# A two-layer diffusion step on one core: DeltaNet rounds whose TensorE order is written down, and a first norm from token-major square sums

## The chip, the cores and the metric

The kernel runs on one core of a Trainium2 chip. The metric is the device time of one launch in microseconds; smaller is better. TensorE (PE in the profile, its weight loads PEld), VectorE (DVE), ScalarE (ACT), GpSimd (POOL) and SyncE (SP, here only a DMA queue) run side by side and wait for each other through semaphores.

## The reference

One inference step of a trunk with two layers over 640 tokens: 128 context tokens and 512 latent tokens, model width 1024. Layer 0 is grouped-query attention, layer 1 is a bidirectional gated DeltaNet with 8 heads; each layer ends in a squared-ReLU MLP. What matters here:

```python
def trunk_layer(x, mods, gain1, gain2, w1, w2, mixer):
    shift1, scale1, gate1, shift2, scale2, gate2 = mods
    mix, aux = mixer(rms_norm(x, gain1) * (1 + scale1) + shift1)
    x = x + gate1 * mix
    h = rms_norm(x, gain2) * (1 + scale2) + shift2
    x = x + gate2 * (jnp.square(jax.nn.relu(h @ w1)) @ w2)
    return x, aux
...
def modulation(cond, w_mod, b_mod):
    m = jax.nn.silu(cond) @ w_mod + b_mod          # w_mod: 1024 x 6144 for each layer
...
def delta_mixer(h, s0, w_in, conv_w, a_log, dt_bias, norm_gain, w_out):
    proj = h @ w_in                                 # q, k, v, z: 8 heads x 128 each
    qkv = silu(centred_depthwise_conv(qkv, conv_w)) # 5 taps
    ...                                             # per head and direction: decay matrices,
    tinv = triangular_solve(eye + lower, eye)       # the inverse of a triangular matrix,
    S, o = lax.scan(step, s0, ...)                  # and a scan over chunks of tokens
```

## The kernel before

Activations stand feature-major: 8 tiles of 128 features by 640 tokens. Every weight and activation that enters a large matmul is split into a rounded part (hi, on ACT) and a rest (lo, on DVE or POOL), and each product is three matmuls (`mm3`). A projection of 128 outputs is done in two halves of 320 tokens, 24 matmuls each (`dense_half`, `dense_steps`).

**Order of the work.** The program is written as generators that `weave` interleaves: it always advances the part whose next step is the smallest share of its declared number of steps. This gives the written order. At build time a planner goes through the instructions with its own costs and puts each engine's instructions in an order: when an engine comes free in its plan, the earliest-written instruction that is ready then goes first. So an engine's order can differ from the written one; on the chip each engine then runs its queue strictly in that order. A `NoSync` edge between two instructions fixes their order on the engine and adds no wait.

**The start** (`run`, stage "ps0"). Five token tiles of `x` (`load_x`, 512 KB each) and then the first third of layer 0's modulation weights (`modulate(0, 0)`: 8 steps of 1 MB, each as four 256 KB pieces into free slots, `fetch_slots`) come over SP's queue. `transpose_x` turns `x` feature by feature on PE, DVE copies it out of PSUM, ACT squares it, DVE adds the squares; then a matmul with a column of ones, a reciprocal square root on DVE (`finish_rstd`) and a broadcast by matmul give the first norm's factor. These steps are written alternately with the 8 modulation steps. `key_weights` loads and splits the key weights (L559) and the first query weight (`q0`). `first_norm` multiplies by the factor (`us`), finishes the modulation, and makes h for three token segments (128, 256, 256 tokens): for every third feature tile on POOL, else on DVE. The key projection then takes one block of 128 tokens after another (24 matmuls each); block 0 needs segment 0, blocks 1 and 2 segment 1, blocks 3 and 4 segment 2.

**The DeltaNet rounds** (`delta`). Round r does, woven together: the projections of head r (`dn_dense`, declared 54 steps of three matmuls, rounds 0 to 7), the decay matrices of head r-1 (`dn_decay`, 20 steps), the inverse of head r-2 (`dn_inverse`, 10 steps), the scan of head r-3 (`dn_scan`, 14 steps), and from round 6 on the z projections (`gated`). Two hand-overs go through DRAM: `dn_decay` computes k times k on PE (its tenth step), DVE makes `gm` of it, writes it out (`gmd`), reads its diagonal blocks back (`ptmp`), solves them in 28 small dependent operations (`ptri`), writes the result (`td`), and `dn_inverse` of the next round reads it with 16 DMAs on SP's queue (`wide`, L1102). The first matmuls of an inverse (`big<-wide,a`) wait for that; they are written as the third of its ten steps. Rounds 8 to 10 have no q, k, v projection.

Of the kernel before, what the change touches and what calls it, by code (L numbers as in the profile page):

```python
# [2 lines left out]

# [5 lines left out]
F32 = mybir.dt.float32  # L9
F32R = mybir.dt.float32r  # L10
I32 = mybir.dt.int32
AF = mybir.ActivationFunctionType
ALU = mybir.AluOpType
AX = mybir.AxisListType

P = 128
# [61 lines left out]
def weave(*parts):  # L78
    live = [[0, n, i, g] for i, (g, n) in enumerate(parts)]
    while live:  # L80
        live.sort(key=lambda e: ((e[0] + 1) / e[1], e[2]))
        e = live[0]
        try:
            next(e[3])
            e[0] += 1
        except StopIteration:
            live.pop(0)
# [5 lines left out]
def pinned(tc, main, n, side, m):  # L93
    nc = tc.nc
    last = {}
    why = mybir.DependencyInfo(mybir.DependencyClass.NoSync, mybir.DependencyReason.DATA)
    traced = lambda i: nc.cur_bb.bb.instructions[i:]
    at = len(traced(0))
    done = step = 0
    for _ in main:  # L100
        step += 1
        for i in traced(at):
            if i.engine in PINNED:
                last[i.engine] = i.name
        at = len(traced(0))
        while done * n < step * m and next(side, True) is None:
            done += 1
            for i in traced(at):
                if i.engine in last:
                    tc.add_manual_dep(i, last[i.engine], why, reason="paced")  # L110
            at = len(traced(0))
    drain(side)


def drain(g):
    for _ in g:
        pass


class Model:  # L120
# [340 lines left out]
            out += [r[:, 0, :], r[:, 1, :]]  # L461
        return out

    def fetch_slots(self, src):
        out = []
        for i in range(4):
            r = self.main("h" if i < 2 else "a", shape=[P, 512])
            self.nc.sync.dma_start(out=r, in_=src[:, i * 512 : (i + 1) * 512])
            out.append(r)
        return out  # L470

    def load_x(self):
# [6 lines left out]
            xs.append(t)  # L479
        return xs  # L480

    def transpose_x(self, xs, x):
        for f in range(FT):
            x.append(self.main("x"))
            ps = self.ps("big", 2, 1024)
            for b in range(NBLK):
                self.tr(ps[:, b * P : (b + 1) * P], xs[b][:, f * P : (f + 1) * P])
            self.nc.vector.tensor_copy(out=x[f], in_=ps[:, :T])
            sq = self.main("x")
            self.act(sq, x[f], AF.Square)  # L490
            if f == 0:
                acc = sq
            else:
                self.tt(acc, acc, sq, ALU.add)
            yield
        cols = self.ps("nps", 1)[:, :NBLK]
        for b in range(NBLK):
            self.mm(cols[:, b : b + 1], acc[:, b * P : (b + 1) * P], self.one_col)
        r = self.finish_rstd(cols)
        out = self.ps("big", 2, 1024)  # L500
        for b in range(NBLK):
            self.mm(out[:, b * P : (b + 1) * P], r[:, b : b + 1].to_broadcast([P, P]), self.ident)
        self.r0 = out[:, :T]
        yield

    def first_norm(self, x, gm):
        us = [self.main("a") for _ in range(FT)]
        for f in range(FT):
            self.tt(us[f], x[f], self.r0, ALU.mult)
        drain(gm)  # L510
        h = self.new_h()
        gain, mods = self.gains[0][0], self.mods[0]
        for s, e, g in FIRST:
            for f, (hi, lo) in enumerate(h):
                eng = self.nc.gpsimd if f % 3 == 2 else self.nc.vector
                u = us[f][:, s:e]
                self.ts(u, u, gain[:, f, g : g + 1], ALU.mult, mods[:, f, g : g + 1], ALU.add, eng=eng)
                self.act(hi[:, s:e], u, AF.Copy)
                self.tt(lo[:, s:e], u, hi[:, s:e].bitcast(F32), ALU.subtract, eng)
        return h  # L520

    def spill(self, x, eng=None):
# [49 lines left out]
    def key_weights(self):  # L572
        v, g = self.nc.vector, self.nc.gpsimd
        self.kw = self.kv_weights(self.kv_raw(QW), lambda: self.wtile([P, 4, 256]), 4, (g, v))
        self.vraws = self.kv_raw(QW + KVH * P)
        self.q0 = self.pair(self.a["attn_w_in"][0], 0, 0, eng=g)

    def attn_kv(self, h, x):
        nc, a = self.nc, self.a
# [181 lines left out]
    def psum(self, name):  # L761
        return self.tc.tile_pool(name=name, bufs=1, space=bass.MemoryType.PSUM)
# [481 lines left out]
    def delta(self, h, first):  # L1244
# [31 lines left out]
        for r in range(HEADS + 3):  # L1276
# [11 lines left out]
                parts.append((self.dn_dense(h, r, first if r == 0 else None), 54))  # L1288
            if r >= HEADS:
                parts.append((islice(wm, MODS[r - HEADS]), MODS[r - HEADS]))  # L1290
            weave(*parts)
        drain(wm)
        self.first = self.prefetch(a["dn_w_out"][0], 0, [f * P for f in range(FT)])
        drain(self.dn_out(HEADS - 1))
# [27 lines left out]
    def run(self):  # L1322
# [1 line left out]
        pool = lambda name: tc.tile_pool(name=name, bufs=1)  # L1324
        psum = self.psum
        FC = [f * P for f in range(FT)]
        with psum("ps0") as self.pq:
            xs = self.load_x()
            self.setup()
            gm = self.modulate(0, 0, self.fetch_slots)  # L1330
            x = []
            tx = self.transpose_x(xs, x)
            for _ in range(FT):
                next(gm)
                next(tx)
            drain(tx)
            self.columns()
            self.key_weights()
            h = self.first_norm(x, gm)
        with pool("attn") as self.ph:  # L1340
            self.attention(h, x)
            first = self.prefetch(a["attn_w_out"][0], 0, FC)
# [126 lines left out]
```

## Time and profile before

| what | value |
|---|---|
| time, median of 3 runs | 1884.3 us (1880.81 to 1886.86) |
| profiled execution: its own time | 1883.34 us |
| profiled execution: span of the instructions | 1881.5 us |
| granted TensorE clock, mean | 0.984 |
| PE busy, share of the span | 95% |
| DMA traffic | 248.84 MB, mean 132 GB/s |

The profile is one execution. Busy time of an engine is the union of its instructions; a matmul's end is modelled, so a busy PE can still lose time between dependent matmuls. "Idle before" is the time an engine stood still just ahead of an instruction, with what ended it. Times in the trace count from the start of the span.

### The profile page before, as it was taken

To read this page: it belongs to the slowest core of one execution; us is meant where nothing else is said; L and a number is where in the kernel's file an instruction comes from. 1 tells how busy PE (TensorE), PEld (TensorE's weight loads), DVE (VectorE), ACT (ScalarE), POOL (GpSimd) and SP (SyncE) were. 2 spreads that over 40 slices of the span, in tenths; PEclk is the share of its full clock that TensorE was granted. 3 is DMA by queue.
4 is the path that set the end of the run, shared out by engine and by line. 5 is a ranking of instruction groups with operands and counts; after the bars stand their busy time and mean duration, and the time that the engine had idled before them with its cause. 6 is when DMAs were issued, how large, how long until landed. Compare 5 with 4: busy or idle time off the path is not lost.

```text
span 1881.5 us, 31040 instructions
## 1 busy us (share of the span) xinstructions
PE 1793.3 (95%) x11981; PEld 1657.3 (88%) x11981; DVE 991.3 (53%) x2294; ACT 753.9 (40%) x1725; POOL 311.6 (17%) x404
## 2 busy tenths in 40 slices
PE   6899999999999999999999999999899999999997
PEld 2778876979999999999898999776699999999997
DVE  4636662724454545556788876543664334343432
ACT  2445552523342433436766555533343223131331
POOL 1344221400010010142121101210251000000012
PEclk9899999999999999999999999999999999999998
DMA  7651127465676676624432332654721222222211
GB/s 279 217 161 49 34 85 219 112 201 165 189 224 196 198 227 180 200 82 165 130 105 81 106 109 85 192 169 143 230 81 48 74 79 74 73 79 75 72 46 56
DMA packets 289065, 248.84 MB, mean 132 GB/s; under 512 B 44847, under 2 KB 246982, under 8 KB 288918
## 3 DMA queue, kind: packets, MB, share of 16 engines
q1 hardware_dynamic: 269072, 207.85, 36.9%
q0 software_dynamic: 9136, 32.18, 4.7%
q10 hardware_dynamic: 10710, 6.83, 1.2%
q8 instruction: 94, 1.54, 0.3%
q14 instruction: 53, 0.43, 0.1%
HBM read 199.00 MB, written 45.20 MB: 130 GB/s over the span
## 4 chain that ended last, share of the span: by engine, by line
PE 75%; DVE 14%; DMA 5%; issue 2%; ACT 2%; POOL 1%; SPq 1%; POOLq 0%; ACTq 0%; DVEq 0%
PE dense L173 32%; PE pd L173 29%; PE scan L173 3%; PE big L173 2%; DVE cv L166 2%; PE mod L408 2%; DVE ptmp L160 2%; PE pd L408 2%; PE big L176 1%; DVE ptri L1069 1%; DVE a L160 1%; DMA raw<-in_w_mod 1%; DVE wide L160 1%; DMA ptmp<-gmd 1%; PE S L173 1%
## 5 line engine op out<-in xcount | busy, mean ns | idle before, releaser
L173 PE MATMUL pd<-h,w 128*128 128x320 f32 x2016 | 353.6, 320 | 10.3 <-ACT cv L163 6.2
L173 PE MATMUL dense<-a,wx 128*128 128x320 f32 x2238 | 338.4, 310 | 2.2 <-ACT wx L163 1.5
L173 PEld LDWEIGHTS dense<-a,wx 128*128 128x128 f32 x2238 | 331.6, 189 | 5.1 <-ACT wx L163 2.4
L173 PEld LDWEIGHTS pd<-h,w 128*128 128x128 f32 x2016 | 301.0, 190 | 37.0 <-issue 21.0
L163 ACT ACTIVATE wx<-raw 128x1024 fp32r<-128x1024 f32 x132 | 139.8, 1059 | 362.5 <-PE dense L173 214.7
L173 PE MATMUL dense<-h,wx 128*128 128x320 f32 x1776 | 266.9, 309 | 0.0
L173 PEld LDWEIGHTS dense<-h,wx 128*128 128x128 f32 x1776 | 261.7, 188 | 5.9 <-issue 5.0
L160 DVE TENSOR_TENSOR wx<-raw,wx 128x1024 fp32r<-128x1024 f32 x127 | 159.1, 1255 | 155.4 <-ACT wx L163 155.4
L173 PE MATMUL pd<-a,wx 128*128 128x320 f32 x1284 | 194.3, 309 | 0.0
L173 PEld LDWEIGHTS pd<-a,wx 128*128 128x128 f32 x1284 | 189.9, 188 | 0.0
L173 PE MATMUL pd<-h,wx 128*128 128x320 f32 x1008 | 152.0, 309 | 0.0
L166 DVE SCALAR_TENSOR_TENSOR x<-dense,c,x 128x192 f32<-128x192 f32 (+2 forms) x147 | 59.6, 433 | 175.3 <-PE dense L173 175.3
L173 PEld LDWEIGHTS pd<-h,wx 128*128 128x128 f32 x1008 | 148.8, 188 | 1.7 <-DVE a L160 1.7
L160 POOL TENSOR_TENSOR x<-x,half 128x320 f32<-128x320 f32 x48 | 54.1, 1127 | 526.1 <-ACT half L163 525.3
L163 ACT ACTIVATE a<-half 128x320 fp32r<-128x320 f32 x128 | 59.9, 471 | 112.5 <-DVE half L166 112.5
L160 DVE TENSOR_TENSOR a<-half,a 128x320 fp32r<-128x320 f32 x128 | 62.7, 492 | 65.2 <-ACT a L163 65.1
L911 POOL DMA_DIRECT2D wd<-w x58 | 31.0, 535 | 369.7 <-ACT w L163 289.8
L166 DVE SCALAR_TENSOR_TENSOR x<-pd,c,x 128x128 f32<-128x128 f32 (+2 forms) x87 | 35.8, 439 | 105.5 <-PE pd L173 105.4
L166 DVE SCALAR_TENSOR_TENSOR cv<-cv,c,cv 128x644 f32<-128x644 f32 x84 | 78.2, 931 | 20.0 <-ACT cv L163 18.9
L163 ACT ACTIVATE half<-x 128x320 f32<-128x320 f32 x56 | 26.0, 468 | 99.8 <-DVE x L166 99.8
L173 PE MATMUL big<-wide,a 128*128 128x128 f32 x480 | 64.4, 281 | 1.0 <-DMA wide<-td 0.8
L173 PEld LDWEIGHTS big<-wide,a 128*128 128x128 f32 x480 | 59.1, 194 | 5.8 <-ACT a L163 2.0
(294 smaller groups left out, 2510.9 us busy)
## 6 DMA issues: line engine op xcount, KB each, us to landing
raw<-in_mlp_w SPq DMA_DIRECT2D x128, 512.0 KB
wd<-w POOLq DMA_DIRECT2D x58, 512.0 KB, 4.4
w<-wd SPq DMA_DIRECT2D x58, 512.0 KB
raw<-in_w_mod SPq DMA_DIRECT2D x48, 512.0 KB
rawp<-in_dn_w_in SPq DMA_DIRECT2D x58, 256.0 KB
a<-in_w_mod SPq DMA_DIRECT2D x48, 256.0 KB
wm<-in_w_mod SPq DMA_DIRECT2D x16, 512.0 KB
raw<-in_attn_w_in SPq DMA_DIRECT2D x12, 512.0 KB
```

The costliest lines, as they stand in the source:

```text
L160: (eng or self.nc.vector).tensor_tensor(out=out, in0=in0, in1=in1, op=op)
L163: self.nc.scalar.activation(out=out, in_=in_, func=func, **kw)
L166: self.nc.vector.scalar_tensor_tensor(out=out, in0=in0, scalar=s, in1=in1, op0=op0, op1=op1)
L173: self.nc.tensor.matmul(out, l, r, start=first, stop=last)
L176: self.nc.tensor.transpose(out, in_, self.ident[:n, :n])
L408: nc.tensor.matmul(ps[32 * q : 32 * q + 32, :], self.cond[:, k, :], views[q], start=k == 0, stop=k == FT - 1, tile_position=(0, 32 * q),)
L911: self.nc.gpsimd.dma_start(out=d[z], in_=pair[z].bitcast(F32).rearrange("p k c -> p (k c)"))
L1069: nc.vector.tensor_reduce(out=t[:, BASE * i : BASE * i + i], in_=o, axis=AX.X, op=ALU.add)
```

## The change

Two separate edits. First, in rounds 1 to 7 every PE instruction gets an ordering edge to the PE instruction written before it in the same round, so PE keeps the written order inside each of these rounds; the other engines are still ordered by the planner, and no edge crosses from one round to the next. Second, the start is rewritten: the square sums are taken from the token-major tiles on ACT with the accumulate output (`token_rstd`), all transposes are written ahead, the modulation matmuls are ordered behind the last PE instruction written up to then (the transposes in `columns`), their weights come in sixteen 512 KB pieces into eleven buffers of a new pool that is closed before the attention's pool opens, h is made without POOL and with scale and shift applied twice (on ACT for the rounded part, on DVE for the rest), and `q0` is loaded and split after `first_norm`, its rest on DVE instead of POOL.

```diff
+@contextmanager
+def in_order(tc, engine):
+    at = len(tc.nc.cur_bb.bb.instructions)
+    yield
+    why = mybir.DependencyInfo(mybir.DependencyClass.NoSync, mybir.DependencyReason.DATA)
+    prev = None
+    for i in tc.nc.cur_bb.bb.instructions[at:]:
+        if i.engine == engine:
+            if prev is not None:
+                tc.add_manual_dep(i, prev, why, reason="as written")
+            prev = i.name
...
-    def fetch_slots(self, src):
+    def fetch_start(self, src):
         out = []
-        for i in range(4):
-            r = self.main("h" if i < 2 else "a", shape=[P, 512])
-            self.nc.sync.dma_start(out=r, in_=src[:, i * 512 : (i + 1) * 512])
-            out.append(r)
+        for i in range(2):
+            r = self.scr("wm", 11, [P, 2, 512])
+            self.nc.sync.dma_start(out=r, in_=src[:, i * 1024 : (i + 1) * 1024].rearrange("p (q c) -> p q c", q=2))
+            out += [r[:, 0, :], r[:, 1, :]]
         return out
...
-    def transpose_x(self, xs, x):
+    def token_rstd(self, xs):
+        ss = self.small("sst", [P, NBLK], 1)
+        for b in range(NBLK):
+            junk = self.scr("junk", 1, [P, D])
+            self.act(junk, xs[b], AF.Square, accum_out=ss[:, b : b + 1])
+        r = self.finish_rstd(ss)
+        out = self.ps("big", 2, 1024)
+        for b in range(NBLK):
+            self.mm(out[:, b * P : (b + 1) * P], r[:, b : b + 1].to_broadcast([P, P]), self.ident)
+        return out[:, :T]
+
+    def transpose_x(self, xs):
+        x = []
         for f in range(FT):
...
             self.nc.vector.tensor_copy(out=x[f], in_=ps[:, :T])
-            sq = self.main("x")
-            self.act(sq, x[f], AF.Square)
-            if f == 0:
-                acc = sq
-            else:
-                self.tt(acc, acc, sq, ALU.add)
-            yield
...
-                eng = self.nc.gpsimd if f % 3 == 2 else self.nc.vector
                 u = us[f][:, s:e]
-                self.ts(u, u, gain[:, f, g : g + 1], ALU.mult, mods[:, f, g : g + 1], ALU.add, eng=eng)
-                self.act(hi[:, s:e], u, AF.Copy)
-                self.tt(lo[:, s:e], u, hi[:, s:e].bitcast(F32), ALU.subtract, eng)
+                sc, sh = gain[:, f, g : g + 1], mods[:, f, g : g + 1]
+                t = self.main("x", shape=[P, 2 * SEQ])[:, : e - s]
+                self.act(hi[:, s:e], u, AF.Identity, scale=sc, bias=sh)
+                self.ts(t, u, sc, ALU.mult, sh, ALU.add)
+                self.tt(lo[:, s:e], t, hi[:, s:e].bitcast(F32), ALU.subtract)
...
-        self.q0 = self.pair(self.a["attn_w_in"][0], 0, 0, eng=g)
...
-            weave(*parts)
+            if 0 < r < HEADS:
+                with in_order(self.tc, PINNED[0]):
+                    weave(*parts)
+            else:
+                weave(*parts)
...
-        with psum("ps0") as self.pq:
+        with pool("start") as self.ph, psum("ps0") as self.pq:
             xs = self.load_x()
             self.setup()
-            gm = self.modulate(0, 0, self.fetch_slots)
-            x = []
-            tx = self.transpose_x(xs, x)
-            for _ in range(FT):
-                next(gm)
-                next(tx)
-            drain(tx)
+            x = self.transpose_x(xs)
+            r0 = self.token_rstd(xs)
             self.columns()
+            tail = lambda: max(i for i, t in enumerate(nc.cur_bb.bb.instructions) if t.engine == PINNED[0])
+            traced = nc.cur_bb.bb.instructions
+            after = traced[tail()]
+            gm = self.modulate(0, 0, self.fetch_start)
+            with tc.issue_after(after):
+                for _ in range(FT):
+                    next(gm)
             self.key_weights()
-            h = self.first_norm(x, gm)
+            h = self.first_norm(x, r0, gm)
+            self.q0 = self.pair(a["attn_w_in"][0], 0, 0)
```

## Rows read from the trace of the kernel before

**Rows 1.** The page: busy time of each engine, share of the span, instructions.

```profile
PE 1793.3 (95%) x11981; PEld 1657.3 (88%) x11981; DVE 991.3 (53%) x2294; ACT 753.9 (40%) x1725; POOL 311.6 (17%) x404
```

**Rows 2.** The page: the chain that ended last, shares of the span by engine.

```profile
PE 75%; DVE 14%; DMA 5%; issue 2%; ACT 2%; POOL 1%; SPq 1%; POOLq 0%; ACTq 0%; DVEq 0%
```

**Rows 3.** Windows of the start: stretch, length, busy by engine, PEclk, DMA share, GB/s.

```profile
0.00:30.00 30.00, 19.81 (x75) 7.32 (x75) 12.40 (x19) 7.50 (x11) 6.52 (x16) 1.00 0.94 345
30.00:35.00 5.00, 4.62 (x18) 1.62 (x17) 2.23 (x13) 0.00 (x0) 0.00 (x0) 0.69 1.08 367
40.00:45.00 5.00, 3.41 (x26) 1.03 (x18) 5.00 (x8) 2.15 (x3) 0.52 (x1) 1.00 0.00 0
45.00:50.00 5.00, 1.21 (x5) 1.21 (x6) 5.00 (x13) 2.13 (x7) 4.80 (x5) 0.56 0.36 114
50.00:55.00 5.00, 3.97 (x19) 3.60 (x18) 5.00 (x11) 3.08 (x10) 4.66 (x8) 0.50 0.95 315
55.00:60.00 5.00, 2.91 (x18) 2.71 (x18) 5.00 (x10) 3.02 (x13) 3.06 (x2) 0.84 1.02 401
60.00:90.00 30.00, 30.00 (x187) 21.90 (x187) 14.08 (x56) 11.68 (x42) 5.04 (x5) 0.96 0.55 169
```

**Rows 4.** Timeline of 41 to 70 us, by engine: start, us, engine, line, operation.

```profile
41.73 1.02 PE L408 MATMUL mod<-a,c 128*32 128x512 f32 x2
...
45.30 1.55 DVE L166 SCALAR_TENSOR_TENSOR c<-c,c,c 128x8 f32<-128x8 f32 x1
...
47.91 0.22 DVE L166 SCALAR_TENSOR_TENSOR c<-c,c,c 128x8 f32<-128x8 f32 x1
48.06 0.84 DVE L170 TENSOR_SCALAR a<-a,c,c 128x128 f32<-128x128 f32 x3
...
58.41 1.76 DVE L160 TENSOR_TENSOR h<-a,h 128x256 fp32r<-128x256 f32 x5
...
47.04 4.35 POOL L170 TENSOR_SCALAR a<-a,c,c 128x128 f32<-128x128 f32 x6 [0.20 <-issue]
...
58.21 11.58 PE L173 MATMUL pd<-w,h 128*128 128x256 f32 x82 [2.09 <-DVE h L160]
```

**Rows 5.** PE's instructions by form, from round 1's start to the first inverse.

```profile
L173 PE MATMUL pd<-h,w 128*128 128x320 f32 x349 | 54.6, 312 | 3.0 <-ACT cv L163 3.0
```

**Rows 6.** Timeline of PE around the first inverse matmuls.

```profile
918.53 9.37 PE L173 MATMUL pd<-h,w 128*128 128x320 f32 x62 [1.10 <-ACT cv L163]
928.74 1.35 PE L173 MATMUL big<-wide,a 128*128 128x128 f32 x10 [0.83 <-DMA wide<-td]
```

**Rows 7.** Windows from 928.7 us, cut where each round's first inverse matmul starts.

```profile
1012.60:1052.20 39.60, 37.52 (x286) 35.70 (x286) 34.29 (x94) 27.77 (x83) 7.12 (x12) 1.00 0.35 97
...
1147.10:1204.20 57.10, 54.25 (x393) 49.83 (x392) 42.17 (x121) 34.28 (x107) 9.11 (x11) 1.00 0.46 140
sum 275.50, PE 261.72 PEld 248.07 DVE 212.76 ACT 165.88 POOL 44.87; mean PE 43.62 PEld 41.34 DVE 35.46 ACT 27.65 POOL 7.48
```

**Rows 8.** PE's projections by form in the same 275 us.

```profile
L173 PE MATMUL pd<-h,w 128*128 128x320 f32 x806 | 151.1, 325 | 3.8 <-ACT cv L163 3.2 <-ACT x L163 0.5
```

**Rows 9.** The chain that ended last: pieces that show PE's undisturbed rates.

```profile
1151.32 1.11 PE big L173 x10
...
1421.89 7.04 PE pd L173 x48
```

**Rows 10.** Timelines of PE and SP: the hand-over from k times k to the inverse.

```profile
1018.16 1.28 PE L173 MATMUL big<-x 128*128 128x128 f32 x10
...
1156.42 1.28 PE L173 MATMUL big<-x 128*128 128x128 f32 x10
...
1204.17 0.38 PE L173 MATMUL big<-wide,a 128*128 128x128 f32 x2
...
1020.40 0.38 SPq L1042 DMA_DIRECT2D gmd<-a  x1
...
1042.06 8.82 SPq L1102 DMA_DIRECT2D wide<-td  x16
```

More of the change, by code (lines that the diff above doesn't have):

```diff
@@ L1 @@
 import math
+from contextlib import contextmanager
 from itertools import islice
@@ L488, in transpose_x, with first_norm @@
             self.nc.vector.tensor_copy(out=x[f], in_=ps[:, :T])
-            sq = self.main("x")
-            self.act(sq, x[f], AF.Square)
-            if f == 0:
-                acc = sq
-            else:
-                self.tt(acc, acc, sq, ALU.add)
-            yield
[L496 to L506, printed above, removed]
+        return x
+    def first_norm(self, x, r0, gm):
         us = [self.main("a") for _ in range(FT)]
         for f in range(FT):
-            self.tt(us[f], x[f], self.r0, ALU.mult)
+            self.tt(us[f], x[f], r0, ALU.mult)
         drain(gm)
```

## The prediction

> **What bounds the kernel now.** I read the page first. PE is busy for 95% of the span and the chain that ended last runs through PE for 75% of it [rows 1, 2], so time can come only from PE standing still or from PE work that goes away; this change takes next to none away. I then cut the two places that it touches into windows. In the start the reader is to see three phases [rows 3]: until about 35 us the DMA engines are full (share 0.94 and above, 345 and 367 GB/s); from 40 to 45 us they move nothing and DVE has no gap; from 45 to 60 us DVE is still full and PE works 1.21, 3.97 and 2.91 us of each five. From 60 us on PE is full. So whatever brings PE's first full stretch forward is worth its time. In the DeltaNet rounds PE is nearly full already: between the first inverse (928.7 us) and the one at 1204.2 us it is idle for 275.5 - 261.7 = 13.8 us by its matmuls [rows 6, 7]. What is left to gain there is small; what the written order costs is the question.
>
> **The start, what it removes.** The w_mod pieces bring 8.39 MB, x 2.62 MB, small tables some 0.3 MB; 345 GB/s for 30 us is 10.35 MB, and the last 0.95 MB at 367 GB/s land at about 32.6 us [rows 3]. Yet the last of their matmuls ends at 42.75 us and the last gain at 48.13 us [rows 4]: ten microseconds after the data, the modulation stood behind the norm's chain (squares, sums, broadcast, eight products on DVE). After the change the squares (five on ACT, off token tiles that land early) and the copies run while DMA is the bound, and nothing of the norm but DVE's products, done by then, stands between the last piece and its matmuls. Removed work (seven adds on DVE, eight squares, five matmul columns) was under the same cover and counts as nothing; without that cover the five squares would cost about 5 us of ACT.
>
> Modulation ready: from the last matmul to the last gain the trace takes 5.4 us, in which one small DVE operation took 1.55 us and its like 0.22 us [rows 4]; I take 4.5 us. Data at 32.6 us at the earliest. SP's queue is the doubt: only eleven buffers hold sixteen pieces, the last five wait for matmuls that now stand behind the transposes in `columns`, and the planner can send ahead of them three pieces of key weights and four tables, 2.3 MB, 6 us at 367 GB/s. I take 35 us, between 33 and 39. Gains then at 39.5 us.
>
> h on DVE alone: 16 operations of 128x128 at about 0.25 us and 32 of 128x256 at about 0.36 us (three took 0.84, five took 1.76 [rows 4]) make 15.5 us, so segment 2 is done at 55 us, and the last key block needs another 24 x 0.141 = 3.4 us (82 in 11.58 [rows 4]): all keys at 58.4 us. Before, 26 of the 120 key matmuls stood before 58.21 us and 94 x 0.141 = 13.3 us after it, 71.5 us. That is 13.1 us earlier. POOL's third of the work (4.35 us for six operations [rows 4]) moves to DVE and is in the sum. `q0` is loaded later and its rest moves to DVE (about 1.25 us); it is not needed before the keys are done. The attention that follows keeps PE busy 30.0 of 30 us from 60 to 90 us, but not everywhere behind that; I let nine tenths through: **-12 us**, ends -5 (pieces held back, h late) and -16 (data at 33 us).
>
> **The rounds, what the written order costs.** Undisturbed, PE does 48 projection matmuls in 7.04 us (0.1467 each) and 10 records of the 128-column products in 1.11 us; each such product is two records, 0.222 us [rows 9]. A full round is 144 x 0.1467 + 84 x 0.222 + 25 transposes x 0.11 = 42.4 us, with a z projection 50.0.
>
> The planner did not keep the written order. From round 1's start to the first inverse PE did 349 projection matmuls [rows 5]; in the written order round 1's 144 and 16 of round 2's steps (0.3 x 54), 48 matmuls, come first, 192 in all. The other 157, 23 us, were done early, and they are what PE did while the first inverse waited for its data: the projections run up to 928 us, and the inverse starts as its DMA lands [rows 6]. With the written order PE reaches that place some 23 us sooner, at about 904 us, and stands there: behind the inverse's first matmul are queued the rest of round 2's projections, and for them wait the convolution and round 3. Nothing can slip past, since round 3's third piece is the scan of the same head. The wait ends where the hand-over ends, 3 us earlier than before I estimate, because fewer convolution taps sit on DVE beside `ptri`.
>
> What is not done early has to be done later. From there to the inverse at 1204.2 us the written order holds 96 + 3 x 144 + 2 x 192 + 30 (z, round 8) = 942 projection matmuls; the trace has 806 [rows 8]. So 136 x 0.1467 = **+20 us** in the same stretch. Against that stands what PE lost there: its work by undisturbed rates is 806 x 0.1467, 480 products of 128 columns x 0.222, 160 transposes x 0.11 and 2 us more, 244 of 275.5 us, so 31 us lost, 13.8 of it shown as idle [rows 7], the rest in dependent little groups. A written order spaces those groups with projections between them. It recovers nothing at the one end and most of the 31 us at the other; with 13 us recovered (the shown idle, the nearest row) the sum is 20 - 13 - 3 = **+4 us**, ends -8 and +20.
>
> By the Trainium skill's Perfetto Trace Analysis, Identifying the Most-Contended Engine, LDWEIGHTS busy time tells more of PE's headroom than matmul time. Here it leaves 275.5 - 248.1 = 27.4 us open [rows 7], nearer to the 31 us than to the 13.8; by it the rounds would come out at -10 instead of +4. No run yet shows that any of it is recoverable by order.
>
> **The sum.** 1883.3 (the profiled execution, 1.8 us of it outside the span) - 12 + 4 = 1875.3; the median of the three runs is 1.0 us above that execution, so **1876 us**.
>
> **Rivals.** *The hand-over sets the round (slower).* From k times k to the next round's inverse the trace takes 34.0 us at the shortest (1018.16 to 1052.2) and 47.8 at the longest (1156.42 to 1204.17); SP alone spends 8.8 us on issuing the 16 reads [rows 10]. In the written order k times k stands a fifth of a round, 9.4 us of PE work, behind the inverse, so a round can't be shorter than 9.4 + hand-over. Before, that distance was only 5.6 us (1012.6 to 1018.16). It decides from a hand-over of 42.4 - 9.4 = 33 us on, so it is near. At 38 us four rounds take 47.4 and two with z 11 + 45 = 56: 302 us against 275.5, less 3, is +23 in the rounds and, with -12, 1894 us. For it: DVE is busy 212.8 of 275.5 us [rows 7]; against it: a stalled PE feeds DVE less, which shortens the hand-over.
>
> *The start gives little (no change).* If SP's order holds back the last w_mod pieces or the planner puts other DVE work ahead of h, the start gives 4 us and the rounds take them: 1883 us. For it: the order of a queue can't be read from this trace; against it: DMA has five idle us at 40 us to give [rows 3].
>
> *The written order recovers most of the loss.* With 26 us recovered the rounds give 9 and the whole 1862 us. Against it: in round 7, where the planner had nothing left to bring forward, a round took 57.1 us [rows 7] for about 50 of work.
>
> *The clock.* PE's granted clock was 0.56 and 0.50 in the windows in which PE had idled most (busy 1.21 of 5 us) and in the next, 0.84 in the third, between its two levels of 1.2 and 2.4 GHz [rows 3]. A wait of 20 us in round 2 would be followed by the same: the 8.1 us of work in those three windows would have taken some 3 to 4 us less at the upper level, so 1879 us, and as much again if later rounds stall. The Trainium skill's Perfetto Trace Analysis, Matmul Optimizations, says that matmuls should be issued back to back in batches because the engine scales with its utilization; holding the projections apart breaks the batches. By that rule the rounds lose more than my +4; the trace agrees as far as the windows above go.
>
> **How the numbers follow.** Forecast (start -9 to -16, rounds -2 to +7; 1868 to 1880): 0.35. Loss recovered (about 1862): 0.15. Start gives little (1881 to 1887): 0.15. Clock (1879 to 1884): 0.08. Hand-over (1888 to 1900): 0.27. This measurement can tell 0.3%, 5.7 us, from no change, so faster ends at 1878.6: most of the forecast (0.32) and all of the recovery, 0.47; the same up to 1889.9: the rest of the forecast, the little start and the clock, 0.26; slower 0.27. The range leaves out the tails of the recovery and of the hand-over: 1860 to 1896.
>
> **What would show it.** Right: the first full PE stretch near 45 us instead of 58 us, no gap of DMA at 40 us, and every PE event of the attention 9 to 14 us earlier; a PE wait of 15 to 23 us on the `wide` reads in round 2 with about 190 projection matmuls ahead of it; first inverses 43 to 46 us apart in rounds 3 to 5. Wrong: if the last w_mod matmul is later than 40 us, the start's term falls; if the inverse of round 2 starts well before 920 us, the hand-over was bound by DVE and the +20 shrinks; if inverses stand 47 us or more apart, the hand-over rival holds.

## The result, and the profile after

The changed kernel takes 1937.68 us (median of 4 runs, 1933.67 to 1945.88) against 1883.05 us (4 runs, 1880.81 to 1886.86): a ratio of 1.0292, 95% interval 1.0266 to 1.0318, so slower. The forecast was 1876 us in a range that ended at 1896; slower had a chance of 0.27, and the rival to which it belonged had put the time at 1894. The profiled execution took 1933.67 us with a span of 1931.9 us and a mean granted clock of 0.972.

The page after, busy time and the chain by engine, beside [rows 1, 2]:

```profile
PE 1791.5 (93%) x11971; PEld 1668.4 (86%) x11971; DVE 999.1 (52%) x2300; ACT 758.7 (39%) x1728; POOL 300.4 (16%) x391
...
PE 72%; DVE 15%; DMA 6%; issue 2%; ACT 2%; SPq 2%; POOL 1%; POOLq 0%; DVEq 0%; ACTq 0%
```

PE's busy time is the same within 2 us in a span that is 50 us longer. The reader is to look for PE standing still, and to be careful with "the same": below, part of that busy time turns out to be slower work.

**The start, after.** Windows, beside [rows 3], and the timeline, beside [rows 4]:

```profile
30.00:35.00 5.00, 3.64 (x22) 0.54 (x14) 3.09 (x5) 0.14 (x1) 0.00 (x0) 1.00 0.92 308
35.00:40.00 5.00, 1.47 (x7) 0.90 (x7) 3.79 (x9) 2.98 (x5) 2.36 (x1) 1.00 0.52 171
40.00:45.00 5.00, 4.47 (x16) 3.33 (x15) 4.38 (x12) 5.00 (x12) 0.00 (x0) 0.55 0.86 271
```

```profile
33.76 1.05 PE L422 MATMUL mod<-wm,c 128*32 128x512 f32 x4 [0.26 <-DMA wm<-in_w_mod]
...
36.42 2.46 DVE L180 SCALAR_TENSOR_TENSOR c<-c,c,c 128x8 f32<-128x8 f32 x2
...
52.58 7.22 PE L187 MATMUL pd<-w,h 128*128 128x256 f32 x58 [1.39 <-ACT blk L177]
60.27 1.05 PE L422 MATMUL S<-raw,c 128*32 128x512 f32 x4 [0.46 <-DMA raw<-in_w_mod]
...
63.86 0.98 PE L187 MATMUL pd<-w,h 128*128 128x256 f32 x6
```

The last w_mod matmul now ends at 34.81 us instead of 42.75 and the last gain at 38.88 instead of 48.13. DMA no longer stops at 40 us. The keys are done at 64.84 us (73.57 before). In the chain of waits a marker just ahead of the DeltaNet stage (two scan transposes) stands at 853.47 us before and at 844.24 us after: 9.2 us, carried through the attention and the first MLP.

**The DeltaNet stage, after.** Windows from that marker to the first 48 projections of the second MLP in the chain; first the kernel before, then the one after (stretch, length, PE busy, PEld, DVE, ACT, POOL, PEclk, DMA share, GB/s):

```profile
853.47:1421.89 568.42, 534.81 (x3692) 481.15 (x3693) 383.10 (x1054) 302.14 (x884) 112.05 (x157) 0.98 0.44 132
```

```profile
844.24:1471.68 627.44, 542.82 (x3692) 495.66 (x3693) 394.52 (x1054) 302.45 (x884) 112.70 (x157) 0.93 0.39 120
```

The same 3692 matmuls take 59.0 us longer. PE's idle time went from 33.6 to 84.6 us (+51.0), its busy time from 534.8 to 542.8 (+8.0), and the granted clock fell from 0.98 to 0.93. Cut into the stretches in which the clock was at its lower level, after has twelve and before four (first and last of the twelve, with the sum):

```profile
859.70:866.50 6.80, 6.21 (x25) 5.60 (x26) 3.20 (x11) 3.25 (x13) 0.00 (x0) 0.50 0.17 61
...
1067.90:1074.70 6.80, 4.25 (x18) 4.28 (x19) 6.19 (x6) 3.14 (x8) 2.13 (x1) 0.50 0.52 162
...
1399.00:1409.20 10.20, 5.75 (x23) 5.75 (x24) 5.83 (x11) 0.74 (x1) 2.31 (x1) 0.50 0.88 288
sum 85.20, PE 54.39 PEld 53.17 DVE 50.44 ACT 32.53 POOL 22.49; mean PE 4.53 PEld 4.43 DVE 4.20 ACT 2.71 POOL 1.87
```

PE worked 54.4 us at a granted clock of 0.50 there. I estimate that 27.2 us of it would not have been needed at the upper level, taking half the clock for twice the time (the inverse's ten records in experiment 5 take 2.13 us at the lower level and 1.10 at the upper, from their start to the next row's). In the kernel before the same sum is 18.3 us, so 9.1. By this estimate the stage's +59.0 us is 51.0 of standing still, 18.1 of slower work, and -10.1 of work that packs more densely (542.8 - 27.2 = 515.6 against 534.8 - 9.1 = 525.7).

**Where PE stands.** The view of waits of PE, stage of the changed kernel (total, times, longest), then the timeline of PE and of SP's queue around one such wait:

```profile
PE big L187 <- DMA wide<-td: 20.4, 4, 6.6
PE big L190 <- POOL a L174: 13.0, 4, 9.2
PE big L187 <- POOL cv L865: 8.6, 1, 8.6
PE scan L187 <- DVE wide L174: 7.9, 4, 3.2
```

```profile
1063.13 0.69 PE L187 MATMUL pd<-h,w 128*128 128x320 f32 x3
1070.45 2.47 PE L187 MATMUL big<-wide,a 128*128 128x128 f32 x10 [6.63 <-DMA wide<-td]
```

```profile
1030.03 0.37 SPq L1053 DMA_DIRECT2D gmd<-a  x1
...
1059.68 0.30 SPq L1095 DMA_DIRECT2D td<-ptu  x1
1061.62 7.48 SPq L1113 DMA_DIRECT2D wide<-td  x16
```

Before, all waits for `wide<-td` in this stage were 0.8 us. Now five first inverse matmuls stand for 8.62, 5.10, 6.63, 6.63 and 2.07 us, 29.0 together. The first is put down to a memset of a convolution buffer at 913.01 us, which the inverse does not read; the 16 reads were issued up to 912.2 us and the inverse began at 913.38, 1.2 us later, as the other four began 1.2 to 1.4 us behind theirs. The chain at each is the one of [rows 10]: k times k, `gmd` out, solve, `td` out, 16 reads, inverse. These waits are 28 of the 51.0 us. Of the rest, PE's waits in the scan grew from 8.0 to 18.7 us and those for GpSimd's `a` from 4.7 to 13.0; experiment 7 bears on them.

The first inverses stand at 913.38, 962.35, 1016.76, 1070.45 and 1125.65 us, 49 to 55 us apart, where the like ones were 40 to 43 us apart before. The round from 1016.76 is read like this: k times k is at 1027.79, 11.0 us behind the inverse; the hand-over from there takes 42.7 us; 11.0 + 42.7 = 53.7, the whole round. For the same head before, that of [rows 10], it was 5.6 + 34.0 = 39.6. Both summands grew, and this head's hand-over grew most: over the four rounds the distance was 5.2 to 6.0 us before and 9.2 to 11.5 after, the hand-over 35.6, 37.2, 34.0 and 38.2 us before and 39.7, 43.5, 42.7 and 43.8 after. The first grew because PE now keeps the written distance. For the second, the timeline of DVE between the `gmd` write and the end of the solve (`ptri`), after:

```profile
1034.03 0.89 DVE L180 SCALAR_TENSOR_TENSOR cv<-cv,c,cv 128x644 f32<-128x644 f32 x1 [1.26 <-ACT cv L177]
...
1041.00 0.89 DVE L180 SCALAR_TENSOR_TENSOR cv<-cv,c,cv 128x644 f32<-128x644 f32 x1
1041.80 0.15 DVE L1076 COPY ptri<-pn 104x1 f32<-104x1 f32 x1
...
1048.25 0.88 DVE L180 SCALAR_TENSOR_TENSOR cv<-cv,c,cv 128x644 f32<-128x644 f32 x1
...
1058.03 0.39 DVE L1080 TENSOR_REDUCE ptri<-ptmp 104x15 f32<-104x225 f32 x1
```

and before:

```profile
1026.08 0.15 DVE L1065 COPY ptri<-pn 104x1 f32<-104x1 f32 x1
...
1036.65 0.39 DVE L1069 TENSOR_REDUCE ptri<-ptmp 104x15 f32<-104x225 f32 x1
```

From `gmd` to the solve's first operation: 5.7 us before (1020.40 to 1026.08), 11.8 after. The solve: 11.0 us before, 16.6 after. Eight convolution taps of 0.88 us, 7.0 us together, stand in that stretch after and none before: they belong to projections that PE now does in the same part of the round as the solve. In the other three rounds four taps stood between k times k and the `td` write before, and eight do after. While PE then waits, DVE has nothing to do (5.07 us idle from 1062.8 us).

### The profile page after: what moved, and what is told of

Same layout as the page of the kernel before. It is cut to its first block, busy times and chain, and to the rows that moved or that the text cites. A ratio compares the mean times of both kernels' runs of the same rounds, so it can differ in the third digit from the quotient of the medians.

```text
span 1931.9 us, 30975 instructions
## 1 busy us (share of the span) xinstructions
PE 1791.5 (93%) x11971; PEld 1668.4 (86%) x11971; DVE 999.1 (52%) x2300; ACT 758.7 (39%) x1728; POOL 300.4 (16%) x391
## 4 chain that ended last, share of the span: by engine, by line
PE 72%; DVE 15%; DMA 6%; issue 2%; ACT 2%; SPq 2%; POOL 1%; POOLq 0%; DVEq 0%; ACTq 0%
PE dense L187 32%; PE pd L187 28%; PE big L187 3%; PE scan L187 3%; DVE cv L180 2%; DVE ptmp L174 2%; PE pd L422 1%; PE mod L422 1%; SPq L1113 1%; DVE ptri L1080 1%; PE big L190 1%; DMA raw<-in_w_mod 1%; DMA wm<-in_w_mod 1%; DVE wide L174 1%; DVE pv L174 1%
## 5 line engine op out<-in xcount | busy, mean ns | idle before, releaser
L187 PE MATMUL pd<-h,w 128*128 128x320 f32 x2016 | 360.2, 325 | 8.1 <-ACT cv L177 3.2
L187 PEld LDWEIGHTS pd<-h,w 128*128 128x128 f32 x2016 | 309.4, 195 | 32.8 <-issue 19.3
L187 PE MATMUL big<-wide,a 128*128 128x128 f32 x480 | 69.8, 297 | 30.7 <-DMA wide<-td 20.4
L187 PEld LDWEIGHTS big<-wide,a 128*128 128x128 f32 x480 | 64.8, 210 | 35.1 <-issue 23.0
L177 ACT ACTIVATE a<-big 128x640 f32<-128x640 f32 x48 | 33.5, 698 | 89.7 <-PE big L187 73.5
```

The costliest lines, as they stand in the source:

```text
L177: self.nc.scalar.activation(out=out, in_=in_, func=func, **kw)
L187: self.nc.tensor.matmul(out, l, r, start=first, stop=last)
```

## The experiments

Medians of all runs; ratios are to the kernel before, run on the same chip, with their 95% interval. No kernel leaves anything of the computation out.

**1. The two edits apart.** First kernel: the changed one with a plain `weave(*parts)` in all rounds. Second: the kernel before with `in_order` around rounds 1 to 7.

> The rewritten start alone, PE free in the rounds. Hand-over theory (in the held rounds PE stands at the first inverse matmuls until the solved blocks are back from DRAM, and nothing behind them can pass) and every other theory that puts the loss into the rounds: the 9 us that the changed kernel still had at the first MLP and at the entry of the DeltaNet stage stay to the end, 1883 - 9 = 1874 us (1868 to 1878). Rival, the start disturbs later stages (its pool, DVE's or ACT's order): 1895 us or more.

> PE held to the written order in rounds 1 to 7, the start as before. Hand-over theory: the changed kernel's 1938 us plus the 9 us that its start gave, 1947 us (1938 to 1953). Rival, the start disturbs later stages: 1890 us or less. If the two edits don't add up, the sum of the two single differences misses +55 us by more than 8 us.

Measured: the start alone 1877.69 us, 0.9965 (0.9952 to 0.9978), a third of a per cent faster and clear of the noise. The order alone 1940.19 us, 1.0286 (1.0258 to 1.0313). In the profiled executions the spans are 1873.2 (-8.3) and 1940.2 (+58.7) and add up to +50.4, which is the +50.4 of both; so exact a match is luck, since by the medians -6.8 and +55.7 make +49.0 where both together made +54.6. That is inside the 8 us that had been set for it. The stage's row of the order alone is that of the changed kernel within a microsecond:

```profile
853.38:1481.41 628.03, 544.54 (x3692) 498.29 (x3693) 395.47 (x1054) 302.85 (x884) 112.56 (x157) 0.93 0.39 120
```

So no run shows the start disturbing anything later, and the loss is the written order's.

**2. The inverse let go, or the projections.** `in_order` skips the PE instructions that one generator wrote:

```diff
+def loose(tc, g, free):
+    bb = tc.nc.cur_bb.bb
+    while True:
+        at = len(bb.instructions)
+        step = next(g, "end")
+        free.update(i.name for i in bb.instructions[at:])
+        if step == "end":
+            return
+        yield
...
-        if i.engine == engine:
+        if i.engine == engine and i.name not in free:
...
-                parts.append((self.dn_inverse(r - 2), 10))
+                parts.append((loose(self.tc, self.dn_inverse(r - 2), self.free), 10))
```

> Both edits, but the inverse's own PE instructions (its transposes and products) get no ordering edge; projections, scan, decay and gates stay in the written order. Hand-over theory: the five waits ahead of a first inverse matmul (8.6, 5.1, 6.6, 6.6 and 2.1 us, 29 us together) and the matmuls at the low clock behind them (some 10 us) go, since projections can pass: 1938 - 39 = 1899 us (1880 to 1908). Rival, many small waits (PE held at every dependent little group, the scan's and the output's transposes): only what the inverse itself adds goes, 1925 us or more.

Measured 1915.77 us, 1.0168 (1.0147 to 1.0188): 22 us back, between the two theories and a miss for both. The waits ahead of the inverse are gone but for the first (11.6 us), yet the rounds still last 48 to 51 us: k times k now follows the inverse by 5.2 to 7.7 us instead of 11, and the hand-over still takes 41 to 45 us; the inverses start 1.1 to 3.0 us behind the issue of their last read. A wait had only moved along the same cycle: I had taken the waits away and forgotten that what they waited for still sets the round.

> Both edits, but the PE instructions of the projections (and of the gates written among them) get no ordering edge; inverse, scan, decay and z projections stay in the written order. Hand-over theory: projections again fill the time in which the inverse waits, so nearly all of the loss returns: 1885 us (1875 to 1895), and over the inverses of rounds 2 to 8 far fewer than 942 projection matmuls stand. Rival, the small groups held in order against each other (scan and output transposes) cost by themselves: 1910 us or more.

The same `loose` around `dn_dense`. Measured 1911.32 us, 1.0162 (1.0128 to 1.0196), where 1885 was expected: a miss. Here 494 projection matmuls of the stage are done by the first inverse and not 336 (by form, from 820 us on), and that wait (8.6 us) is gone; but from the second on the rounds take 48 us, 6.6 us from inverse to k times k and 41.5 us of hand-over. As I read it, filling PE does not shorten a cycle that runs through DVE and DRAM. The cycle is not the whole of it, though: from 967 to 1112 us PE also stands 13.5 us before projections that wait for ACT's `cv`, and one such group, 37 matmuls from 1008.68 us, stands ahead of an inverse whose last read had been issued 3.7 us before it began. Which of the two costs what was not tried.

**3. The cycle's first summand.** One number in the `weave` call writes the whole decay, with k times k in it, earlier in the round:

```diff
-                parts.append((self.dn_decay(r - 1), 20))
+                parts.append((self.dn_decay(r - 1), 30))
```

> Both edits, the decay's 20 steps declared as 30, so that k times k is written at a third of the round instead of a half, some 7 us of PE work earlier. Hand-over theory: a round is the written distance from the inverse to the next k times k (11 us measured) plus the hand-over (42 to 44 us); the distance falls to some 4 us, the round from 54 us to PE's own 47 us, and the waits before the inverse (29 us) and most of the slow matmuls behind them go: 1905 us (1895 to 1915). Rival, the hand-over is bound by DVE's other work, which does not move: it grows by what k times k gains, 1930 us or more. Rival, many small waits: 1930 to 1940 us.

> Both edits with the decay's 20 steps declared as 40, k times k written at a quarter of the round, about where the inverse's first matmuls are. Hand-over theory: at 30 the waits ahead of the inverses of heads 1 to 5 were gone, and only that of head 0 (15 us) and the output's (9 us) were left, so nothing more comes back: 1900 us, within 6. Rival, the hand-over still bounds: 1890 us or less. Rival, what DVE has to do by then is not ready (gm waits for the exponentials): 1908 us or more.

Measured: 1900.14 us with 30, 1.0094 (1.0074 to 1.0115), and 1905.99 with 40, 1.0136 (1.0106 to 1.0165). As expected: 38 us come back with 30, and nothing more with 40 (6 us less than with 30, just inside the bound). In the trace with 30, k times k follows the inverse by 1.7 us (954.4 to 956.1) and the round is bounded by PE itself (windows from one first inverse to the next):

```profile
954.40:999.80 45.40, 44.09 (x337) 42.82 (x338) 36.01 (x101) 25.47 (x82) 5.72 (x11) 1.00 0.38 107
```

against 54.41 us with 45.03 us of PE work, and a clock of 0.94, for the like round of the changed kernel. The clock stays at its upper level (1.00), and PE stands for 1.3 us of that round. With 40 the number came out as expected but not for the expected reason: the data are there early (the reads ahead of the inverse at 1002.68 us were issued up to 992.5), yet three inverses stand 9.8 us together for a product on GpSimd (`a<-a,lev`), and the two rounds behind 952.22 us take 50.5 and 51.0 us. So this run does not tell what a still shorter distance would give.

**4. The cycle's second summand.** The solve ahead of the convolution's taps on DVE (the solve in one piece, and every tap written behind it ordered behind it):

```diff
+        self.solved = max(i for i, t in enumerate(nc.cur_bb.bb.instructions) if t.engine == PINNED[1])
...
+                for i in traced[self.solved + 1 :]:
+                    if i.engine == PINNED[1] and i.name in dense:
+                        self.tc.add_manual_dep(i, traced[self.solved].name, why, reason="solve first")
```

> Both edits; on DVE the convolution taps that are written behind a round's small solve are ordered behind it, and the solve is written in one piece (PE's order and work are as in the changed kernel). Hand-over theory, with DVE as the cause of its length: the solve takes 11 to 12 us instead of 16.6, the hand-over falls from 43 to 38 us and five rounds with it, 22 us together: 1915 us (1905 to 1923), inverses 49 us apart. Rival, the taps are needed sooner than the solve (PE then waits for the projections' buffers instead) or the length is the trip through DRAM: 1933 us or more.

Measured 1919.77 us, 1.0189 (1.0161 to 1.0218): 18 us back, inside the range. The solve takes 12 us (1022.3 to 1034.2), the hand-over of the four rounds 36.7, 38.4, 38.8 and 42.9 us, and the inverses stand 44.5, 47.9, 49.6 and 53.1 us apart. From k times k to the `td` write, the part that runs through DVE, those four took 22.8 to 25.0 us, against 28.9 to 32.7 in the changed kernel and 20.2 to 25.4 before. DVE's order is what made the hand-over long.

Half of the reads over ACT's queue:

```diff
-                nc.sync.dma_start(out=dst, in_=ap)
+                (nc.scalar if n else nc.sync).dma_start(out=dst, in_=ap)
```

> Both edits; the 16 reads of the solved blocks go half over SP's queue and half over ACT's, side by side. Hand-over theory: the last read is issued some 3.7 us sooner (16 took 7.5 us), in five rounds 18 us: 1920 us (1912 to 1928). Rival, ACT stands at the head of its queue until the solved blocks are in DRAM and its own work comes that much later: 1935 us or more.

Measured 1930.63 us, 1.0249 (1.0223 to 1.0274): 7 us back, in the direction of the theory, but less than half of its 18 and outside its range. The issue of the 16 reads fell from 7.5 to about 4 us as expected, and the waits ahead of the first four inverses from 27.0 to 15.7 us (6.26, 1.75, 3.67 and 4.00). So 11 of those 27 us are gone there, but not all of it reached the end; the output's transposes, for one, waited 11.0 us and not 9.2. The sign that the rival named is there as well: ACT stood for its own half of the reads for 27 us in eight waits, and in the changed kernel not once. How much of the missing 11 us that took was not tried.

**5. The clock.** Work put into the waits:

```diff
+            if n == 0 and hd < 4:
+                for _ in range(8):
+                    self.mm(ps[:, T : T + 384], self.ident, v[:, :384])
             for m, s in enumerate(self.blocks()):
                 self.mm(ps[:, s], gl[:, s], self.vview(tm, b, m))
```

> Both edits, and eight extra matmuls of 384 columns (about 5 us of PE work whose result nothing reads) ahead of the first inverse matmuls of the first four heads, where PE stood for 8.6, 5.1, 6.6 and 6.6 us. Hand-over theory: PE only does them while it would wait, the time stays at 1938 us, within 4. Clock theory (a good part of the loss is work at the lower clock behind those waits): the granted clock of the rounds rises and the time falls by 8 us or more, 1930 us or less. If the waits were not where the profile puts them: +20 us.

Measured 1929.22 us, 1.0259 (1.0234 to 1.0284). PE does more work and the kernel is 8.5 us faster. The timeline of PE at the third of the four, first in the changed kernel, then here (the extra work is the row with 384 columns), and the stage's window here:

```profile
1016.76 2.47 PE L187 MATMUL big<-wide,a 128*128 128x128 f32 x10 [6.63 <-DMA wide<-td]
1018.89 2.10 PE L187 MATMUL pd<-h,w 128*128 128x320 f32 x9
```

```profile
1009.50 5.32 PE L187 MATMUL big<-x,c 128*128 128x384 f32 x16
1016.07 1.35 PE L187 MATMUL big<-wide,a 128*128 128x128 f32 x10 [1.24 <-issue]
1017.17 1.57 PE L187 MATMUL pd<-h,w 128*128 128x320 f32 x9
```

```profile
845.44:1465.17 619.73, 557.25 (x3757) 502.73 (x3757) 394.27 (x1054) 302.68 (x884) 112.06 (x157) 0.95 0.40 122
```

The inverse's ten records take 1.35 us here, and the nine projections behind them 1.57; behind the idle wait they took 2.47 and 2.10. The mean clock went from 0.93 to 0.95 and, by windows cut as above, the time at the lower level from 85 to 58 us. The hand-overs stayed within 1.2 us of those of the changed kernel, while the distance from inverse to k times k fell from 9.2 to 11.5 us to 8.8 to 9.5: the faster work shortens the cycle's first summand. So the clock is a real part of the loss, as its rival said, and an effect of the waits: 8.5 us for four of them.

**6. The same levers without the held order.** The start alone with 30 for the decay, and the start alone with the solve first:

> The rewritten start with PE free in the rounds and the decay's 20 steps declared as 30. Hand-over theory: with PE free to pass the wait the hand-over costs little, so its earlier start gives little: 1874 us (1868 to 1880) against 1877.7 for the start alone. Rival, the hand-over bounds the free rounds too (they took 41 to 44 us with 43 us of hand-over): 5 us or more for each of four to six rounds, 1855 us or less.

> The rewritten start, PE free in the rounds, and on DVE the solve ahead of the convolution taps written behind it, as in the run with both edits. Hand-over theory: with PE free, PE's work is the bound and a shorter hand-over gives nothing: 1877.7 us, within 5. Rival, the hand-over bounds the free rounds too: 1865 us or less.

Measured: 1877.57 us, 0.9974 (0.9952 to 0.9995), as expected; and 1895.83 us, 1.0064 (1.0045 to 1.0083), a miss by 18 us on the slow side. The first says that with PE free an earlier k times k gains nothing in the whole. As I read it, a free PE is bound by its own work; but its trace also shows the distance falling from 5 to 6 us to 1.1 and the hand-over growing from 34 to 39 us to 39 to 40, so that a part of the gain was taken there. The second says nothing about the hand-over, because the edit brought a wait of its own (PE's waits in that stage):

```profile
PE big L201 <- ACT x L188: 16.3, 1, 16.3
```

The taps, held back behind a solve, make a convolved tile of the next head late (ACT's last step on it), and its transposes stand for it at 907.9 us.

**7. What is left of the loss with 30: 22 us.** Its trace shows 15.2 us before the first inverse and 8.9 us before an output transpose that waits for GpSimd. First PE was held only in rounds 3 to 7 (`if 2 < r < HEADS`), with 30:

> Both edits with the decay's steps declared as 30, and PE held only in rounds 3 to 7 (rounds 1 and 2 free). Hand-over theory: with 30 the rounds from 3 on no longer waited, and what was left of the loss, 1900 - 1878 = 22 us, is the first wait (15 us idle before the inverse of round 2) that projections of later rounds filled when PE was free: 1880 us (1872 to 1890). Rival, what was left is spread over all the held rounds: 1893 us or more.

Measured 1908.26 us, 1.0134 (1.0111 to 1.0157): a miss, and slower than holding all of them. PE's waits show why:

```profile
PE big L187 <- DMA wide<-td: 17.6, 2, 13.2
```

The wait in the free round 2 is still there, 13.2 us. By then 435 projection matmuls were done, 99 more than in the changed kernel: the 96 that round 2 still had, and 3. As I read it, the rest would have to come from round 3, whose chain has the scan that needs this very inverse near its head. A held round thus reaches back into the free one before it. Then, with 30 and all rounds held, the projections, the outputs (`gated`), or both were let go with `loose`:

> Both edits, decay's steps declared as 30, and the projections' PE instructions without ordering edges. With 30 alone 1900 us, and its trace still shows 15 us idle before the inverse of round 2 and 9 us before an output transpose. If the loss is a sum of such waits at the head of PE's queue, projections fill the first one and it goes: 1885 us (1878 to 1892). Rival, freed projections lengthen the hand-over through DVE's order as they did without the 30: 1897 us or more.

> Both edits, decay's steps declared as 30, and the PE instructions of the z projections and the output transposes without ordering edges. Sum of waits: the 9 us before the output transpose that stood behind GpSimd's multiply go, with some 2 us of work at the low clock behind it: 1889 us (1884 to 1895). Rival, another wait takes its place: 1897 us or more.

> Both edits, decay's steps declared as 30, projections and outputs free; only scan, decay and inverse are held to their written order. Sum of waits: both waits go and nothing of the loss is left, as with the start alone: 1877 us (1870 to 1884). Rival, 10 us or more of the loss belong to the small groups held in order: 1888 us or more.

Measured: 1882.37 us, 0.9991 (0.9969 to 1.0013); 1885.25 us, 1.0005 (0.9986 to 1.0025); 1879.12 us, 0.9980 (0.9959 to 1.0002), all three inside their ranges. Each alone gives most of the 22 us back (18 and 15), both 21, back to the start alone within 1.4 us. So nothing is left for the small groups as such: scan, decay and inverse in written order cost nothing that these runs can tell. The parts overlap, and the reason is only partly seen: with the outputs free the first wait is still 15.2 us long,

```profile
PE big L198 <- DMA wide<-td: 15.2, 1, 15.2
```

and the time comes back in the last rounds instead, where k times k of the last head is at 1210.8 us and not at 1228.2.

None of these beats the start alone, 1877.69 us (1877.57 with 30 is the same within the noise), which beats both kernels.

## Why the prediction was wrong, point by point

**The start's term, -12 us (-5 to -16): right in mechanism, a little large.** Data at 35 us (34.8 measured), gains at 39.5 (38.9) and h by 55 us (56.8) held. The keys did not end at 58.4 us but at 64.8: I had let the last key block run alone, while matmuls of the next modulation third, which wait for their own DMAs at 60.27 and 62.88 us, stand between its pieces and take 3 us with their waits. The rest is h, 1.8 us late, and 39 instead of 24 key matmuls that were left by then. The same modulation work stood between the keys before, where I had left it out too, so that they ended at 73.57 us and not at 71.5:

```profile
72.47 1.10 PE L173 MATMUL pd<-w,h 128*128 128x256 f32 x7
```

The keys came 8.7 us earlier instead of 13.1. 9.2 us reached the DeltaNet stage, and the start alone is worth 6.8 us in the median and 8.3 in the profiled span.

**192 projections by the first inverse: right, the wait behind them too long.** From round 1's first projection to the first inverse (by form, 855.8 to 913.3 us):

```profile
L187 PE MATMUL pd<-h,w 128*128 128x320 f32 x192 | 33.1, 333 | 0.0
```

against 349 in [rows 5]. PE stood from 904.8 us, and the wait ended at 913.4: 8.6 us, not the 15 to 23 that I had named as a sign. The count behind the +20 us held as well: from there to the inverse of head 6 at 1255.7 us the trace has 961 projection matmuls, where I had 942 and the trace before 806.

**The failed step: "It recovers nothing at the one end and most of the 31 us at the other; with 13 us recovered ... +4 us".** The written order was to remove PE's idle time in the later rounds. It made it two and a half times as long: 33.6 to 84.6 us in the stage. What I had taken from [rows 7] were two different losses. The one between dependent little groups did shrink, by 10.1 us as estimated above; that this is near the 13 is chance, since the 13 was taken from the other one. The shown idle, from which I took that number, is what the planner's freedom had kept small, and the order that was to remove it made it. In its place the runs show the round as a cycle through the hand-over, with inverses 49 to 55 us apart where I had forecast 43 to 46; in the sum it had no term, since I had argued it away as a rival. The Trainium skill's Perfetto Trace Analysis, Identifying the Most-Contended Engine, judges PE's headroom by the busy time of its weight loads, and from the 27.4 us that this left open I had worked out -10 for the rounds. The trace does not bear my -10 out: the stage lost 59 us with that headroom open.

**"The wait ends ... 3 us earlier, because fewer convolution taps sit on DVE beside `ptri`": right at the first inverse, the wrong sign in every round behind it.** The first inverse starts 69.1 us behind the stage's marker and not 75.3, with ten taps instead of 15 between its k times k and its `td` write. I had priced only that place. In the full rounds eight taps stand in the hand-over in place of one to four, and it grew by 4 to 9 us. I had argued from what PE no longer does early and did not ask where in the round it does it instead. Ordering the solve first gave 18 us back.

**The hand-over rival: right in mechanism, priced too low.** I wrote "a round can't be shorter than 9.4 + hand-over" and took 38 us for it, with inverses 47.4 us apart; 11.0 + 42.7 = 53.7 is what the trace shows. It had its own test, inverses 47 us or more apart, and passed it with 49 to 55. Its bound had been met from the start: it was to decide from a hand-over of 33 us on, and every hand-over of the trace before was longer, from 34.0 to 50.3 us (878.48 to 928.74, not 47.8 as I had written for the longest). It was refuted in my text by "a stalled PE feeds DVE less, which shortens the hand-over". PE does stall, and DVE idles with it, but after the solve, not before it. The two summands were shown apart: the distance (38 us back with 30) and the length (18 us with the solve first).

**The clock rival: right, and too small alone.** I gave it 3 to 4 us per wait and 0.08. It cost 18.1 us in the stage by the estimate above; four waits filled with work gave 8.5 us. The Trainium skill's Perfetto Trace Analysis, Matmul Optimizations, says that matmuls should be issued back to back in batches; the trace agrees, with 54.4 us of PE work at a granted clock of 0.50 in twelve stretches where there were 18.3 in four.

**What no step named.** PE's output transposes stood 9.2 us behind a GpSimd multiply:

```profile
1171.66 1.26 POOL L174 TENSOR_TENSOR a<-a,rsy 128x640 f32<-128x640 f32 x1 [0.77 <-DVE ng L184]
...
1172.97 1.33 PE L190 MATMUL big<-c,a 128*128 128x128 f32 x5 [9.22 <-POOL a L174]
```

The multiply itself had waited for `rsy`, a reciprocal square root in small operations that DVE did from 1165.85 to 1171.52 us between the solve's copies, a tap and work of another head. A free PE had waited 1.5 us at most for such a multiply. Any dependence in the held order can become such a wait, since nothing can pass it.

## What to carry to other kernels

When a loop is a cycle through other engines and DRAM, price a written order by the cycle (distance between its two matmuls in the written order, plus the trip between them), not by the sum of PE's work; and price the trip with the work that the new order puts beside it on the other engines, since it is not the trip of the old trace. If an order must be held, write the start of the trip early: one declared step count gave back 38 of the 60 us here. PE paid twice here for standing still: 51.0 us of idle time and, by the estimate above, 18.1 us of slower work.

## What was not expected of the hardware

Added work made the kernel faster: 32 extra matmuls of 384 columns in four waits took 8.5 us off (1937.68 to 1929.22), the time at the lower clock going from 85 to 58 us. The 16 reads of the solved blocks took 7.5 us to issue on one queue and about 4 us as eight on each of two, and only 7 us of the kernel followed.
